# State-space recurrence of a hybrid encoder layer: one vector operation for both directions instead of two, and a lower pace of it beside keys, values and gate projections

## The chip, the cores and the metric

The kernel runs as one program on one core of a Trainium2 chip. Four engines matter here: TensorE (PE, matrix products, with its weight loads PEld), VectorE (DVE), ScalarE (ACT) and GpSimd (POOL); SyncE (SP) only issues transfers. The metric is the device time of one execution in microseconds; the median over several executions is compared.

## The reference, cut to what matters

One layer with 256 tokens and width 2048. Everything hangs on one input projection; the part that the change touches is the two-directional state-space recurrence (S5).

```python
h = rms_norm(x, mix_norm_g[l])
proj = h @ w_in[l]
q, k, v, u, gate_a, gate_b = jnp.split(proj, IN_SPLITS, axis=-1)
...
y_a = windowed_gqa(q, k, v, attn_sink[l]) @ w_attn_o[l]
ug = u.astype(jnp.float32).reshape(b_, s_, SSM_GROUPS, SSM_GROUP)
y_fwd = s5_direction(ug, ..., False)
y_bwd = s5_direction(ug, ..., True)
y_ssm = (y_fwd + y_bwd).reshape(b_, s_, SSM_WIDTH) + ssm_d[l] * ug.reshape(b_, s_, SSM_WIDTH)
y_act = jax.nn.gelu(y_ssm, approximate=False)
y_b = (y_act @ glu_w_a[l]) * jax.nn.sigmoid(y_act @ glu_w_b[l])
merged = jax.nn.sigmoid(gate_a) * y_a + jax.nn.sigmoid(gate_b) * y_b
x = x + merged @ w_out[l]
...
x = x + peer(h2, peer_w_query[l], ...)
```

Inside `s5_direction` every group has 64 complex states; a state at one time is a diagonal complex factor times the state before it, plus a driving term from `u`. The forward direction runs up the time axis, the other one down.

## The kernel before, in words

**Products.** All big weights are streamed from memory in pieces of 128x1024 (`raw`, four buffers). Each piece is split into a high part `whi` (ACT, `high_part`, line 151) and a low part `wlo` (DVE, `low_part`, line 136; two buffers each). `dense` (lines 284 to 288) then issues twelve products of 512 columns per piece: eight with `whi`, and four with `wlo`. I call the work on one such piece a half; eight halves make 512 columns of a weight matrix. The input projection has 16 such blocks, 128 halves: two of `u`, one of keys, one of values, four of queries, eight of gates. After it come the attention's output matrix (`w_ao`), the gated unit, `w_out`, the query projection of the expert layer, and two long passes over all experts.

**The recurrence.** Time is folded by two, so that 128 positions with 128 states per partition are left. The state tile is `X`, with index [direction][real, imaginary][32 groups][129 positions]; neighbours in a group index lie 129 words apart. `ssm` fills it (`ssm_bu`, 16 pairs of groups: transposes and products on PE, one half of the copies on ACT and one on DVE, line 612), and then makes 127 steps. In a step, for each direction: `s1` = state times real factor (`lr2`), `s2` = swapped state times imaginary factor (`li2`), then the new column gets `s1` and `s2` added. The trace calls both products `s`. One such operation has 64 elements per partition, two runs of 32 that hop 129 words from element to element. Eight such operations make a step, and the forward and backward ones alternate. Behind the steps the output products (lines 696 and 699, from `X`, `ccl` and `Tm`) make the state-space output, ACT applies the GELU, and POOL's queue moves it. The tile `ysp` then takes the place of `X` in memory: the split of the attention's result (`att_split`, tiles `attl` to `ysp`) has to wait until the last output product has read `X`, and `w_ao` needs that split.

**What sets the order.** The recurrence is a generator in the list `fill`. `dense` calls `pump(budget)` after each half: the budget is added to a credit, and generators are advanced until it is used up; a recurrence step costs 1.0. The budget is 2.5 in the blocks of `u`, `SPK` in those of keys and values, `SPU` = 1.2 in those of queries and `SPG` in those of gates. Ahead of the last gate block `drain` takes out whatever is left. That gives the order in which instructions are written; a scheduler then places them on each engine by priority and its own estimate of durations, the two splits of a weight piece 400 places earlier than written (`HP`). So the final order on an engine is not the written one. On each engine instructions start in that final order.

Of the kernel before, what the change touches and what calls it, by code (L numbers as in the profile page):

```python
# [17 lines left out]
OP = mybir.AluOpType  # L18
AX = mybir.AxisListType

P = 128
# [10 lines left out]
NG2 = 32  # L32
# [78 lines left out]
def _layer(ctx: ExitStack, tc: tile.TileContext, a, out):  # L111
# [17 lines left out]
    def mm_ps():  # L129
        return psm.tile([P, 512], F32, name="mm", tag="mm")  # L130

    def ax_ps():
        return psx.tile([P, 512], F32, name="ax", tag="ax")

    def tt(o, i0, i1, op, eng=None):
        return (eng or V).tensor_tensor(o, i0, i1, op=op)  # L136
# [10 lines left out]
    def act(o, i, f, **kw):  # L147
        S.activation(o, i, f, **kw)
# [36 lines left out]
    for i2 in range(2):  # L185
        for q in range(2):
# [4 lines left out]
                                      ap=[[0, P], [1, HEADS]]))  # L191
# [82 lines left out]
    def dense(w, cc, lh, ll, ps, budget=0.0, early=(), keep=False):  # L274

        nu = 2 * w.shape[1]
        parts = (p for m in range(nu // 2)
                 for p in split_units(unit(w, cc, m), early[m] if m < len(early) else ()))
        for un, (hi, lo) in enumerate(parts):
            kb = [(j, b) for j in range(2) for b in range(NB)]  # L280
            for j, b in kb:
                k = 2 * un + j
                h_, bs = hi[:, j * 512:(j + 1) * 512], slice(b * P, (b + 1) * P)
                PE.matmul(ps[b], lhsT=lh[:, k, bs], rhs=h_, start=(k == 0), stop=False)  # L284
                PE.matmul(ps[b], lhsT=ll[:, k, bs], rhs=h_, start=False, stop=False)  # L285
            for j, b in kb:
                k = 2 * un + j
                PE.matmul(ps[b], lhsT=lh[:, k, b * P:(b + 1) * P], rhs=lo[:, j * 512:(j + 1) * 512],  # L288
                          start=False, stop=(k == 2 * nu - 1))
            step()  # L290
            pump(budget)
        if keep:
            return
        flush()
# [7 lines left out]
    def tmp(shape, dt=F32, name="t8_"):  # L302
        return t8.tile(shape, dt, name=name, tag="t8")
# [60 lines left out]
    lr2 = ss.tile([P, 2, 2, NG2], F32, name="lr2")  # L364
    li2 = ss.tile([P, 2, 2, NG2], F32, name="li2")
# [122 lines left out]
    XW = P + 1  # L488
# [97 lines left out]
    def ssm_bu(X):  # L586
        ready = []
        for ip in range(17):
            if ip < 16:
                e, pl = ip // 2, ip % 2  # L590
                bp = ax_ps()
                for d in range(2):
                    for ri in range(2):
                        PE.transpose(bp[:, (2 * d + ri) * P:(2 * d + ri + 1) * P],
                                     bws[e][:, ri, d, 2 * pl:2 * pl + 2, :].rearrange("p i c -> p (i c)"), ident)
                bt = bts[ip % 2]
                for i2 in range(2):
                    hs = slice(i2 * 64, (i2 + 1) * 64)
                    copy(bt[i2][hs].rearrange("p k n -> p (k n)"), bp[hs])
                if pl == 1 and e < 8 - NBW:  # L600
                    load_bw()
                ready.append(bt)
            if ip > 0:
                for i2 in range(2):
                    i = 2 * (ip - 1) + i2
                    sp = ax_ps()
                    for k in range(4):
                        PE.matmul(sp[:, k * P:(k + 1) * P], lhsT=ready[ip - 1][i2][:, k, :], rhs=uT[:, ip - 1, :],
                                  start=True, stop=True)
                    spv = sp.rearrange("p (d r t) -> p d r t", d=2, r=2)  # L610
                    copy(X[:, 0, :, i, 1:1 + P], spv[:, 0])
                    V.tensor_copy(X[:, 1, :, i, 0:P], spv[:, 1])
            yield 0.5
# [26 lines left out]
    def ssm():  # L640
        Xf = pp.tile([P, XN], F32, name="X", tag="X")
        X = Xf.rearrange("p (d r i t) -> p d r i t", d=2, r=2, i=NG2)
        for d in range(2):
            nc.gpsimd.memset(X[:, d, :, :, d * P:d * P + 1], 0.0)
        yield from ssm_bu(X)
        dm = tmp([P, 16, P], name="dm")
        tt(dm, ident.unsqueeze(1).to_broadcast([P, 16, P]), dd.unsqueeze(2).to_broadcast([P, 16, P]), OP.mult)
        Tf = Tm.rearrange("p a b c -> p a (b c)")
        tt(Tf, Tf, dm, OP.add)
        yield 4.6  # L650
        base = X.offset
        pst = list(X.ap[0])
        SR = NG2 * XW

        def view(d, j, swap):
            return bass.AP(tensor=X.tensor, offset=base + 2 * d * SR + j + (SR if swap else 0),
                           ap=[pst, [-SR if swap else SR, 2], [XW, NG2]])

        s12 = ss.tile([P, 2, 2, 2, NG2], F32, name="s12")
        s1, s2 = s12[:, 0], s12[:, 1]  # L660
        ccl = []

        def load_cc():
            t_ = ss.tile([P, 2, 2, 4, 64], F32, name="ccl", tag="bw", bufs=NBW)
            nc.gpsimd.dma_start(t_.rearrange("p r d i c -> p (r d i c)"), cc_d[len(ccl)])
            ccl.append(t_)

        for _ in range(NBW):
            load_cc()
        for j in range(1, P):  # L670
            dirs = range(2)
            cu = [X[:, d, :, :, (j + 1, P - 1 - j)[d]] for d in dirs]
            pr_, sw = ([view(d, (j, P - j)[d], w_) for d in dirs] for w_ in (False, True))
            for d in dirs:
                tt(s1[:, d], pr_[d], lr2[:, d], OP.mult)
            for d in dirs:
                tt(s2[:, d], sw[d], li2[:, d], OP.mult)
            for d in dirs:
                tt(cu[d], cu[d], s1[:, d], OP.add)
            for d in dirs:  # L680
                tt(cu[d], cu[d], s2[:, d], OP.add)
            yield 1.0
        for _ in range(8):
            yield None
        Y = tmp([P, 16, P], name="Y")
        for e in range(8):
            cc_ = ccl[e]
            yp = ax_ps()
            for pl in range(2):
                ip = 2 * e + pl  # L690
                o = yp[:, pl * P:(pl + 1) * P]
                for i2 in range(2):
                    hs = slice(i2 * 64, (i2 + 1) * 64)
                    for n in range(4):
                        d, ri = n // 2, n % 2
                        PE.matmul(o[hs], lhsT=cc_[:, ri, d, 2 * pl + i2, :],
                                  rhs=X[:, d, ri, 2 * ip + i2, d:d + P], start=(n == 0), stop=False,
                                  tile_position=(0, i2 * 64), skip_group_check=True)
                PE.matmul(o, lhsT=Tm[:, ip].rearrange("p b c -> p (b c)"), rhs=uT[:, ip, :],
                          start=False, stop=True, skip_group_check=True)  # L700
            if e < 8 - NBW:
                load_cc()
            act(Y[:, 2 * e:2 * e + 2, :].rearrange("p a t -> p (a t)"), yp[:, :T], AF.Gelu)
            yield 2
        sp_ = pp.tile([P, 56, T], F32, name="ysp", tag="X")
        split.append(sp_)
        ya = sp_[:, 48:56, :]
        for i4 in range(4):
            for s_ in range(2):
                p0 = (i4 % 2) * 64 + s_ * 32  # L710
                nc.gpsimd.dma_start(ya[i4 * 32:(i4 + 1) * 32, :, s_ * P:(s_ + 1) * P],
                                  Y.rearrange("p (e q) t -> p e q t", q=2)[p0:p0 + 32, :, i4 // 2, :])
# [105 lines left out]
        nc.gpsimd.dma_start(att_d[:, g * 4 * T:(g + 1) * 4 * T], w2[:, 1])  # L818

    SPU = 1.2  # L820
    SPK = 1.8
    SPG = 2.2
    def values(ps):
        for b in range(NB):
            copy(vv[:, b, :], ps[b], scale=rstd[:, b:b + 1])
        yield

    def queries(g, ps):
        qT = tmp([P, 4, T], name="qT")
        yield from head_norm(ps, gq, qT)  # L830
        yield from attend(g, qT)

    for n in range(2 + KV):
        ps = [mm_ps(), mm_ps()]
        dense(a["w_in"], 2 + n, hh, hl, ps, SPK if n < 2 else SPU)
        front.append(head_norm(ps, gk, kT) if n == 0 else values(ps) if n == 1 else queries(n - 2, ps))
# [17 lines left out]
    for gi, dst in enumerate((sga_d, sgb_d)):  # L854
        for cc in range(4):
# [6 lines left out]
            ps = [mm_ps(), mm_ps()]  # L862
            dense(a["w_in"], 8 + gi * 4 + cc, hh, hl, ps, SPG)
            sg = tmp([P, NB, 512], name="sg")
# [27 lines left out]
    for cc in range(4):  # L892
# [11 lines left out]
        for b in range(NB):  # L904
            o = mg[b][:, cc * 512:(cc + 1) * 512]
# [9 lines left out]
    for cc in range(4):  # L915
# [3 lines left out]
        for b in range(NB):  # L919
            o = x1[b][:, cc * 512:(cc + 1) * 512]  # L920
# [32 lines left out]
    pr_ = ExitStack()  # L953
# [397 lines left out]
    for h in range(2):  # L1351
# [11 lines left out]
        for c in range(NK):  # L1363
# [41 lines left out]
            for i in range(8):  # L1405
                rh, rl = region(i)
                o = ot[:, i, NGT:]
# [29 lines left out]
```

## Time and profile before

| | us |
|---|---|
| median of 3 executions (2312.93 to 2314.45) | 2313.37 |
| the profiled execution, own time | 2316.0 |
| its span in the trace | 2314.2 |
| PE busy (share of the span) | 2242.6 (97%) |
| DVE busy | 1833.0 (79%) |
| ACT busy | 1218.2 (53%) |
| POOL busy | 312.5 (14%) |

Read the shares as averages over stages. PE is near its whole span in all of them, but a product that waits for its `wlo` shows only part of its wait as idle time, since products overlap; the distance from one half's last product to the next half's last product tells more than the busy share. DVE is far from busy in some stages and has no idle time at all in another.

### The profile page before, as it was taken

To read this page: it belongs to the slowest core of one execution; us is meant where nothing else is said; L and a number is where in the kernel's file an instruction comes from. 1 tells how busy PE (TensorE), PEld (TensorE's weight loads), DVE (VectorE), ACT (ScalarE), POOL (GpSimd) and SP (SyncE) were. 2 spreads that over 40 slices of the span, in tenths; PEclk is the share of its full clock that TensorE was granted. 3 is DMA by queue.
4 is the path that set the end of the run, shared out by engine and by line. 5 is a ranking of instruction groups with operands and counts; after the bars stand their busy time and mean duration, and the time that the engine had idled before them with its cause. 6 is when DMAs were issued, how large, how long until landed. Compare 5 with 4: busy or idle time off the path is not lost. (4 is left out here: it accounts for less than half of the span.)

```text
span 2314.2 us, 37265 instructions
## 1 busy us (share of the span) xinstructions
PE 2242.6 (97%) x13298; PEld 1996.1 (86%) x13298; DVE 1833.0 (79%) x4154; ACT 1218.2 (53%) x2090; POOL 312.5 (14%) x309
## 2 busy tenths in 40 slices
PE   7999899999999999999989999999999999999999
PEld 6788676678888888888879999999999999999998
DVE  7858999964466575999979999999778888875665
ACT  5885654334344554455445555555555555545554
POOL 3320000001000100000021222112323323200000
PEclk9999999999999999999999999999999999999999
DMA  6854345566666765555577677777888888876664
GB/s 236 263 186 137 128 137 170 171 224 193 223 204 203 239 214 188 178 191 185 186 244 247 241 243 252 248 241 258 291 319 305 300 313 306 290 229 218 206 209 156
DMA packets 145466, 519.05 MB, mean 224 GB/s; under 512 B 18032, under 2 KB 18656, under 8 KB 144896
## 3 DMA queue, kind: packets, MB, share of 16 engines
q1 hardware_dynamic: 113184, 410.04, 52.8%
q0 software_dynamic: 30944, 105.56, 13.0%
q8 instruction: 104, 1.70, 0.3%
q10 hardware_dynamic: 1152, 1.07, 0.1%
q14 instruction: 82, 0.67, 0.1%
HBM read 496.11 MB, written 18.87 MB: 223 GB/s over the span
## 5 line engine op out<-in xcount | busy, mean ns | idle before, releaser
L151 ACT ACTIVATE whi<-raw 128x1024 fp32r<-128x1024 f32 x768 | 814.6, 1061 | 933.4 <-PE mm L285 225.8
L136 DVE TENSOR_TENSOR wlo<-raw,whi 128x1024 fp32r<-128x1024 f32 x768 | 938.4, 1222 | 395.8 <-ACT whi L151 379.0
L1293 PE MATMUL mm<-h,whi 128*128 128x448 f32 x2048 | 478.9, 370 | 0.0
L1293 PEld LDWEIGHTS mm<-h,whi 128*128 128x128 f32 x2048 | 367.5, 190 | 22.7
L1300 PEld LDWEIGHTS mm<-h,wlo 128*128 128x128 f32 x2048 | 265.5, 191 | 33.2 <-DVE wlo L136 26.2
L1300 PE MATMUL mm<-h,wlo 128*128 128x224 f32 x2048 | 272.5, 275 | 14.4 <-DVE wlo L136 14.2
L1384 PE MATMUL mm<-wt,whi 128*128 128x448 f32 x1024 | 252.2, 367 | 4.0 <-DVE wt L136 4.0
L284 PE MATMUL mm<-whi,hb 128*128 128x512 f32 x512 | 204.4, 401 | 9.5 <-ACT hb L151 8.2
L285 PE MATMUL mm<-whi,hb 128*128 128x512 f32 x512 | 202.8, 398 | 0.3 <-DVE hb L145 0.2
L1384 PE MATMUL ax<-wt,whi 128*128 128x448 f32 x768 | 198.2, 365 | 0.0
L1384 PEld LDWEIGHTS mm<-wt,whi 128*128 128x128 f32 x1024 | 174.5, 190 | 15.1 <-issue 3.3
L1186 POOL DMA_INDIRECT rows<-in_down_rows_dram,rix x64 | 107.4, 1678 | 396.6 <-DVE dots L1194 389.4
L288 PE MATMUL mm<-wlo,hb 128*128 128x512 f32 x512 | 148.2, 406 | 10.1 <-DVE wlo L136 9.9
L1387 PE MATMUL ax<-wt,wlo 128*128 128x224 f32 x1024 | 156.8, 275 | 0.0
L1387 PE MATMUL mm<-wt,wlo 128*128 128x224 f32 x1024 | 156.4, 275 | 0.0
L1384 PEld LDWEIGHTS ax<-wt,whi 128*128 128x128 f32 x768 | 144.1, 188 | 10.2
L1387 PEld LDWEIGHTS mm<-wt,wlo 128*128 128x128 f32 x1024 | 144.9, 191 | 4.0
L1387 PEld LDWEIGHTS ax<-wt,wlo 128*128 128x128 f32 x1024 | 135.8, 193 | 0.0
L288 PEld LDWEIGHTS mm<-wlo,hb 128*128 128x128 f32 x512 | 92.9, 189 | 44.2 <-DVE wlo L136 26.3
L284 PEld LDWEIGHTS mm<-whi,hb 128*128 128x128 f32 x512 | 97.1, 190 | 32.0 <-ACT hb L151 8.6
L285 PEld LDWEIGHTS mm<-whi,hb 128*128 128x128 f32 x512 | 96.7, 190 | 20.3 <-DVE hb L145 1.1
L136 DVE TENSOR_TENSOR X<-X,s 128x64 f32<-128x64 f32 x508 | 107.1, 278 | 0.0
(276 smaller groups left out, 3224.0 us busy)
## 6 DMA issues: line engine op xcount, KB each, us to landing
raw<-in_down_dram SPq DMA_DIRECT2D x256, 512.0 KB
raw<-in_up_dram SPq DMA_DIRECT2D x256, 512.0 KB
raw<-in_w_in_dram SPq DMA_DIRECT2D x128, 512.0 KB
raw<-in_w_ao_dram SPq DMA_DIRECT2D x32, 512.0 KB
raw<-in_w_out_dram SPq DMA_DIRECT2D x32, 512.0 KB
raw<-in_w_q_dram SPq DMA_DIRECT2D x32, 512.0 KB
raw<-in_wgb_dram SPq DMA_DIRECT2D x16, 512.0 KB
raw<-in_wga_dram SPq DMA_DIRECT2D x16, 512.0 KB
```

The costliest lines, as they stand in the source:

```text
L136: return (eng or V).tensor_tensor(o, i0, i1, op=op)
L151: S.activation(o, i, AF.Copy, **kw)
L284: PE.matmul(ps[b], lhsT=lh[:, k, bs], rhs=h_, start=(k == 0), stop=False)
L285: PE.matmul(ps[b], lhsT=ll[:, k, bs], rhs=h_, start=False, stop=False)
L288: PE.matmul(ps[b], lhsT=lh[:, k, b * P:(b + 1) * P], rhs=lo[:, j * 512:(j + 1) * 512], start=False, stop=(k == 2 * nu - 1))
L1186: nc.gpsimd.indirect_dma_start(out=r[:PU], out_offset=None, in_=table, in_offset=bass.IndirectOffsetOnAxis(ap=rix[:PU, h, g:g + 1], axis=0))
L1293: PE.matmul(ps[:, :2 * ND], lhsT=hi[:, j * P:(j + 1) * P], rhs=h2[:, k].rearrange("p a t -> p (a t)"), start=(k == 0), stop=(k == KD - 1), ...
L1300: PE.matmul(ps[:, :ND], lhsT=lo[:, j * P:(j + 1) * P], rhs=h2[:, q * 8 + j, 0, :], start=False, stop=False, skip_group_check=True)
L1384: PE.matmul(acc[i][:, :2 * ND], lhsT=w_, rhs=wv, start=first, stop=False, skip_group_check=True)
L1387: PE.matmul(region(i)[0], lhsT=lo[:, i * P:(i + 1) * P], rhs=wh, start=False, stop=end, skip_group_check=True)
```

## The change

Each recurrence step is now four operations of 128 elements instead of eight of 64: `view` builds one access pattern over both directions (the forward column `j` and the backward column `P - j`, 128x2x64 in the order listings). The three arithmetic steps are the same. `SPK` goes from 1.8 to 1.5 and `SPG` from 2.2 to 1.7.

```diff
-        def view(d, j, swap):
-            return bass.AP(tensor=X.tensor, offset=base + 2 * d * SR + j + (SR if swap else 0),
-                           ap=[pst, [-SR if swap else SR, 2], [XW, NG2]])
+        def view(j, swap):
+
+            o = (j, P - j)
+            return bass.AP(tensor=X.tensor, offset=base + o[0] + (SR if swap else 0),
+                           ap=[pst, [2 * SR + o[1] - o[0], 2], [-SR if swap else SR, 2], [XW, NG2]])
...
         for j in range(1, P):
-            dirs = range(2)
-            cu = [X[:, d, :, :, (j + 1, P - 1 - j)[d]] for d in dirs]
-            pr_, sw = ([view(d, (j, P - j)[d], w_) for d in dirs] for w_ in (False, True))
-            for d in dirs:
-                tt(s1[:, d], pr_[d], lr2[:, d], OP.mult)
-            for d in dirs:
-                tt(s2[:, d], sw[d], li2[:, d], OP.mult)
-            for d in dirs:
-                tt(cu[d], cu[d], s1[:, d], OP.add)
-            for d in dirs:
-                tt(cu[d], cu[d], s2[:, d], OP.add)
+            cu, pr_, sw = view(j + 1, False), view(j, False), view(j, True)
+            tt(s1, pr_, lr2, OP.mult)
+            tt(s2, sw, li2, OP.mult)
+            tt(cu, cu, s1, OP.add)
+            tt(cu, cu, s2, OP.add)
             yield 1.0
...
     SPU = 1.2
-    SPK = 1.8
-    SPG = 2.2
+    SPK = 1.5
+    SPG = 1.7
```

The order on DVE in the middle of the gate blocks, from the 101st `wlo` on (`s_2058` is the scratch tile of both products, `li_143` and `lr_142` are the factors; "waits DVE" is a wait for an earlier result of DVE itself). Before:

```order
L136 TENSOR_TENSOR wlo<-raw,whi 128x1024 [waits DMAHW4_49,PE_49,Activation_49]
L136 TENSOR_TENSOR s_2058<-X,li_143 128x64
L136 TENSOR_TENSOR X<-X,s_2058 128x64 [waits DVE_49] x4
L136 TENSOR_TENSOR s_2058<-X,lr_142 128x64 [waits DVE_49] x2
L136 TENSOR_TENSOR s_2058<-X,li_143 128x64 x2
L136 TENSOR_TENSOR X<-X,s_2058 128x64 [waits DVE_49] x4
L136 TENSOR_TENSOR wlo<-raw,whi 128x1024 [waits DMAHW5_49,PE_49,Activation_49]
```

The same place of the changed kernel (scratch tile `s_2207`):

```order
L136 TENSOR_TENSOR wlo<-raw,whi 128x1024 [waits DMAHW4_49,PE_49,Activation_49]
L136 TENSOR_TENSOR s_2207<-X,li_143 128x128
L136 TENSOR_TENSOR X<-X,s_2207 128x2x64 [waits DVE_49] x2
L136 TENSOR_TENSOR s_2207<-X,lr_142 128x128 [waits DVE_49]
L136 TENSOR_TENSOR s_2207<-X,li_143 128x128
L136 TENSOR_TENSOR X<-X,s_2207 128x2x64 [waits DVE_49]
L136 TENSOR_TENSOR wlo<-raw,whi 128x1024 [waits DMAHW5_49,PE_49,Activation_49]
L136 TENSOR_TENSOR X<-X,s_2207 128x2x64 [waits DVE_49]
```

About one and a half steps stand between two `wlo` in both. What moved is the neighbourhood: an addition to `X` now stands right behind the addition whose result it reads, and the next step's product right behind that; before, an operation of the other direction stood between.

The order on PE where the recurrence hands over to the output products (`ax<-X,ccl`; `mm<-wlo,hb` are the four last products of a half of the input projection). Before:

```order
L288 MATMUL mm<-wlo,hb 128x512 [waits DVE_49]
L288 MATMUL mm<-wlo,hb 128x512 x3
L696 MATMUL ax<-X,ccl 64x128 [waits DMASW1_49,DVE_49,Pool_49]
L696 MATMUL ax<-X,ccl 64x128
L696 MATMUL ax<-X,ccl 64x128 [waits DVE_49,Pool_49]
L696 MATMUL ax<-X,ccl 64x128 x5
L699 MATMUL ax<-uT,Tm 128x128
```

In the changed kernel (eight products with `whi` are cut to their first and last here by the "..." line):

```order
L288 MATMUL mm<-wlo,hb 128x512 x2
L692 MATMUL ax<-X,ccl 64x128 [waits DMASW1_49,DVE_49,Pool_49]
L288 MATMUL mm<-wlo,hb 128x512
L284 MATMUL mm<-whi,hb 128x512 [waits Activation_49]
...
L285 MATMUL mm<-whi,hb 128x512
L692 MATMUL ax<-X,ccl 64x128 [waits DVE_49]
L692 MATMUL ax<-X,ccl 64x128 [waits Pool_49]
L692 MATMUL ax<-X,ccl 64x128 x5
L695 MATMUL ax<-uT,Tm 128x128
```

Counted from the start, 118 halves stand ahead of the first output product before, and 123 halves and the eight `whi` products of the next one ahead of the second output product now; the eight groups of output products have two halves mixed in before and stand in one run now. The recurrence's first step stands behind the 39th `wlo` on DVE before and behind the 43rd now; its last step behind the 119th before and behind the 125th now. Behind `w_ao` the orders of both kernels are the same again.

## Rows read from the trace of the kernel before

**Rows 1.** The page: busy us of each engine.

```profile
PE 2242.6 (97%) x13298; PEld 1996.1 (86%) x13298; DVE 1833.0 (79%) x4154; ACT 1218.2 (53%) x2090; POOL 312.5 (14%) x309
```

**Rows 2.** Stretches: length, busy PE PEld DVE ACT POOL (instructions), clock, DMA.

```profile
190.40:380.00 189.60, 172.48 (x744) 131.33 (x743) 188.58 (x787) 108.72 (x250) 4.29 (x8) 0.98 0.40 136
380.00:495.40 115.40, 105.44 (x419) 75.47 (x417) 115.40 (x456) 41.86 (x43) 3.21 (x6) 1.00 0.52 175
495.40:553.60 58.20, 58.20 (x410) 48.49 (x410) 23.28 (x36) 21.78 (x34) 10.03 (x18) 1.00 0.65 217
553.60:640.00 86.40, 86.40 (x383) 71.57 (x382) 43.49 (x40) 34.47 (x35) 5.36 (x10) 1.00 0.69 225
```

**Rows 3.** DVE in order of time, gate blocks: start, us, instruction, count.

```profile
489.63 1.20 DVE L136 TENSOR_TENSOR wlo<-raw,whi 128x1024 fp32r<-128x1024 f32 x1
490.76 0.79 DVE L136 TENSOR_TENSOR X<-X,s 128x64 f32<-128x64 f32 x4
491.48 0.43 DVE L136 TENSOR_TENSOR s<-X,lr 128x64 f32<-128x64 f32 x2
...
492.90 0.25 DVE L136 TENSOR_TENSOR s<-X,lr 128x64 f32<-128x64 f32 x1
493.08 1.20 DVE L136 TENSOR_TENSOR wlo<-raw,whi 128x1024 fp32r<-128x1024 f32 x1
```

**Rows 4.** PE in order of time: last four products of two neighbouring halves, twice.

```profile
487.62 1.19 PE L288 MATMUL mm<-wlo,hb 128*128 128x512 f32 x4 [0.43 <-DVE wlo L136]
...
490.89 1.19 PE L288 MATMUL mm<-wlo,hb 128*128 128x512 f32 x4 [0.25 <-DVE wlo L136]
...
541.78 1.07 PE L288 MATMUL mm<-wlo,hb 128*128 128x512 f32 x4
...
544.50 1.07 PE L288 MATMUL mm<-wlo,hb 128*128 128x512 f32 x4
```

**Rows 5.** DVE groups by form, 0 to 820 us: busy, mean ns, idle before.

```profile
L136 DVE TENSOR_TENSOR X<-X,s 128x64 f32<-128x64 f32 x508 | 107.1, 278 | 0.0
L136 DVE TENSOR_TENSOR s<-X,lr 128x64 f32<-128x64 f32 x254 | 58.4, 270 | 0.0
...
L136 DVE TENSOR_TENSOR prm<-prm 128x64 f32<-128x64 f32 x24 | 5.0, 221 | 0.1
```

**Rows 6.** DVE in order of time, parameters: chain of three, then two independent ones.

```profile
25.21 0.74 DVE L145 SCALAR_TENSOR_TENSOR prm<-prm 128x64 f32<-128x64 f32 x3
...
51.16 0.22 DVE L136 TENSOR_TENSOR prm<-prm 128x64 f32<-128x64 f32 x1
51.29 0.22 DVE L136 TENSOR_TENSOR prm<-lam,prm 128x64 f32<-128x64 f32 x1
...
55.51 0.29 DVE L136 TENSOR_TENSOR stg<-stg 128x128 f32<-128x128 f32 x1
55.71 0.29 DVE L145 SCALAR_TENSOR_TENSOR stg<-stg 128x128 f32<-128x128 f32 x1
```

**Rows 7.** DVE in order of time, expert pass: a hopping operation and its successor.

```profile
1302.24 0.68 DVE L136 TENSOR_TENSOR A<-A,ax 128x260 f32<-128x260 f32 x1
1302.82 1.23 DVE L136 TENSOR_TENSOR wlo<-raw,whi 128x1024 fp32r<-128x1024 f32 x1
```

**Rows 8.** DVE groups by form, 1300 to 2000 us: busy, mean ns, idle.

```profile
L136 DVE TENSOR_TENSOR A<-A,ax 128x124 f32<-128x124 f32 x1 | 0.4, 394 | 0.0
...
L136 DVE TENSOR_TENSOR A<-A,ge 128x128 f32<-128x128 f32 x2 | 0.6, 287 | 0.0
```

**Rows 9.** In order of time: `Tm`, first step, first output product, first of `w_ao`.

```profile
152.41 2.29 DVE L136 TENSOR_TENSOR Tm<-Tm,dm 128x2048 f32<-128x2048 f32 x1 [5.32 <-DMA Tm<-stg]
...
190.39 0.44 DVE L136 TENSOR_TENSOR s<-X,lr 128x64 f32<-128x64 f32 x2
...
495.46 1.58 PE L696 MATMUL ax<-X,ccl 128*64 128x128 f32 x16
...
553.57 0.39 PE L284 MATMUL mm<-whi,ysp 128*128 128x512 f32 x1
```

## The prediction, made before the changed kernel ran

> **What bounds the kernel now.** I read the page's busy times first: PE is busy for 97% of the span [rows 1], so a change on DVE can only help where PE waits for DVE. I then cut the span into stretches [rows 2]. From the first recurrence step to the first output product, 190.4 to 495.4 us, DVE has next to no idle time (188.58 of 189.6 us, 115.40 of 115.4), while PE makes 744 and 419 products. Right behind it, in 553.6 to 640, the same kind of product runs at 383 in 86.4 us, that is 226 ns each; in 380 to 495.4 it is 275 ns. The granted clock is 0.98 and 1.00 there, so the clock is not the reason. In PE's order of time the distance from one half to the next is 490.89 - 487.62 = 3.27 us with a wait for `wlo` in front, and 544.50 - 541.78 = 2.72 us where DVE has time [rows 4]. So the input projection's middle is bound by DVE, about 0.6 us in each gate half, and from 495.46 on PE sets the end: the first product of `w_ao` comes at 553.57 [rows 9] without a gap, and nothing behind it differs between the kernels. What I have to find is when that product starts now.
>
> **What one operation costs.** In the gate blocks a step runs from 491.48 to 492.90 us, 1.42 us, and the four additions before it take 491.48 - 490.76 = 0.72 [rows 3]: eight operations, so 0.176 us from start to start. Each lasts 270 to 278 ns by itself [rows 5]; neighbours overlap by about 0.1. The overlap ends when an operation reads what the one in front of it wrote. In the chain of three, (0.74 - 0.22) / 2 = 0.26 us lie between two starts; the same size without such a wait starts 51.29 - 51.16 = 0.13 later [rows 6]. A direct dependence costs 0.13 us.
>
> The price of 128 hopping elements isn't in the trace. Contiguous operations go from 0.13 us at 64 elements to 55.71 - 55.51 = 0.20 at 128 and 490.76 - 489.63 = 1.13 at 1024 [rows 3, 6], that is 0.069 us plus 1.04 ns an element. The hopping one has 0.176 at 64. If the extra 0.04 us belongs to the operation, 128 elements cost 0.176 + 0.064 = 0.240 us; if it belongs to the elements, (0.176 - 0.069) / 64 = 1.67 ns each, they cost 0.282. A third row reads and writes with a hop of 224 words: 260 elements take 1302.82 - 1302.24 = 0.58 us [rows 7], 1.97 ns each, which gives 0.321. That one also reads another memory (`ax` lies in PSUM), and its hop is another. That the extra grows with the elements is shown by the forms: 124 hopping elements last 394 ns, 128 contiguous ones 287 [rows 8], twice the 57 ns by which 278 exceeds 221 at 64 [rows 5]. I take 0.282, worked out from the recurrence's own operations, and keep 0.240 and 0.321 as ends.
>
> **The recurrence, before and after.** Up to the first output product DVE makes 126 of the 127 steps before: 1008 x 0.176 = 177.4 us. Now the second output product waits for the last step, since its wait for DVE stands behind that step in the order: 508 x 0.282 = 143.3 us. Each step has two direct dependences, addition behind addition and next product behind that, 253 in all. In the order on DVE something else (mostly a `wlo` or a piece of a head norm) stands between 64 of the pairs; 189 x 0.13 = 24.6 us remain. Together 167.9, a gain of 9.5 us. So halving the operations gives little: about 34 us come off, and 25 go back into waits that the other direction used to fill.
>
> **What else moves on DVE between the first step and that product.** 82 `wlo` instead of 79, 3 x 1.13 = +3.4; `dm` and `Tm` fall into the stretch, as long as the row of `Tm` [rows 9] less the overlap, 2 x 2.2 = +4.4; four more gate pieces and one head norm fewer, about -1, an estimate. Sum +6.8. The stretch was 495.46 - 190.39 = 305.1 us [rows 9]; now 305.1 + 6.8 - 9.5 = 302.4.
>
> **When it starts.** The lower `SPK` puts four more halves ahead of the first step (43 `wlo` instead of 39). PE is the bound there, so 4 x 2.72 = 10.9 us later: 201.3. The head norm of the first query group, a chain of small operations that read each other, now stands ahead of the last four copies into `X`; I add 2 us for it, between 0 and 4. Start 203.3, end 505.7.
>
> **What PE has left then.** Before, from 495.46 to 553.57: 58.1 us for ten halves and the output products. Now 123 halves and two thirds of one are done instead of 118: 5.67 x 2.72 = 15.4 us less, so 42.7. The first product of `w_ao` starts at 548.4 instead of 553.57, **5.2 us earlier**. Halves in the stretch are paid either at PE's price or hidden behind DVE; both kernels have DVE full over it, since 1.5 steps x about 1.32 + 1.13 = 3.1 us a half is still over 2.72. That is why the lower pace alone is worth nearly nothing here: the order has about 1.5 steps between two `wlo` in both kernels, because the scheduler, not the budget, spaces them while DVE has a backlog.
>
> At the hand-over the split of the attention's result must wait for the last output product. Behind that only 4.3 halves, 11.8 us, are left as cover, eight halves before. The split's first quarter needs one ACT copy and one DVE subtraction of the size of a `wlo`, some 2.5 us. I cost it at nothing; without cover it would be up to 5 us. What is late next is then the state-space output's way through POOL's queue; 32 halves of `w_ao` hide it.
>
> The sum is made on the profiled execution, 2316.0 us with a span of 2314.2, 2.6 above the median. 5.2 us less are 2310.8 there, and **2308.2** on the median.
>
> **The rivals.**
> *The element price is higher.* At 0.321 us an operation the recurrence costs 508 x 0.039 = 19.8 us more, 14.6 us slower in all: 2328. It decides at 0.292 (no change) and 0.301 (slower by over 0.2%). For it speaks the only other hopping row [rows 7]; against it, that this row reads PSUM, and that both kinds of recurrence operation, one with a hop on one side and one on two, cost the same at 64.
> *The pieces cancel.* With an operation at 0.288 to 0.300, or a start two microseconds later still, the sum is within 0.2%: about 2313.
> The Trainium skill has a rule on this, "Vector Engine (DVE) Microarchitecture Reference", section 5.2 "Measured stream behaviour on trn2": about 75 ns an instruction, 1.04 ns a column, and 1.71 to 1.76 when a source or the destination hops on every element. By that 128 elements would cost an estimated 0.296 us and the change would come out 2 us slower, that is no change; at 64 it gives 186 ns where the rows show 176.
> *The extra belongs to the operation.* At 0.240 us, 508 x 0.042 = 21.3 us come off besides: 2287. The forms speak against it [rows 8].
> *The wait isn't paid.* If the additions overlapped in spite of the dependence, 24.6 us more: 2284. The chain of three speaks against it [rows 6].
> *The hand-over isn't covered.* 5 us given back: 2313.
>
> **How the numbers follow.** The forecast, with an operation between 0.270 and 0.288 us, has 0.45: 2302 to 2311, and 2308 as its number. Cancelling or an uncovered hand-over 0.24; the higher price 0.21; the two cheap cases together 0.10, mostly part of the way. Faster by over 0.2%, 4.6 us, about what a measurement of this kernel can tell from no change: 0.41 of the forecast's 0.45 and the cheap cases, 0.50. Within: 0.04 and 0.23, 0.27. Slower: 0.23. The range leaves out the far half of the cheap cases and of the dear one: 2296 to 2322.
>
> **What would show it.** DVE's groups by form: 508 operations of 128 elements with a mean near 0.38 us. In order of time, a step without anything between at 4 x 0.282 + 0.26 = 1.39 us, with visible gaps of about 0.03 in front of the second addition and the next product, and starts 0.41 apart there. The gate halves on PE at 3.1 to 3.2 us instead of 3.3. The first output product that waits near 506 us, `w_ao` near 548. I am wrong if the two starts around a pair of neighbours lie over 0.30 apart, if the step is over 1.45 us, if DVE shows idle time between 203 and 505, or if PE waits for ACT in front of `w_ao`.

## The result and the profile after

The changed kernel takes 2331.2 us (median of 5 runs, 2325.48 to 2332.22), beside 2314.45 for the kernel before (5 runs, 2312.93 to 2318.48). The ratio is 1.0062 with a 95% interval of 1.005 to 1.0075: **slower by 0.6%**. The forecast was 2308.2, its range ended at 2322. The profiled execution has a span of 2329.5 us, 15.3 more than before.

The page's busy times in the changed kernel, to be read against [rows 1]:

```profile
PE 2249.5 (97%) x13298; PEld 2000.2 (86%) x13298; DVE 1834.9 (79%) x3646; ACT 1217.1 (52%) x2090; POOL 310.8 (13%) x309
```

DVE issues 508 instructions less and is busy for as long as before. The windows of the changed kernel, by the stretches of [rows 2] and with one of six microseconds at the end of the recurrence (length, busy PE, PEld, DVE, ACT, POOL with instructions, clock, DMA share, GB/s):

```profile
190.40:380.00 189.60, 171.34 (x756) 131.15 (x756) 182.15 (x467) 107.95 (x248) 4.85 (x9) 0.97 0.40 131
380.00:495.40 115.40, 101.83 (x408) 73.65 (x407) 111.17 (x237) 40.76 (x43) 4.30 (x8) 1.00 0.53 175
520.00:526.00 6.00, 6.00 (x26) 4.17 (x26) 2.49 (x5) 1.17 (x2) 0.00 (x0) 0.61 0.59 196
553.60:640.00 86.40, 86.40 (x392) 71.64 (x392) 49.32 (x51) 39.63 (x46) 11.15 (x20) 1.00 0.72 228
```

From 380 to 495.4 us PE makes 408 products where it made 419. DVE shows idle time now, 4.2 us in that stretch and 7.4 in the one before, though nothing else bounds it: 237 instructions with gaps took the place of 456 without. Behind the stretch PE is as full as before.

DVE's groups by form, which answer to [rows 5] (busy, mean ns of one, idle before):

```profile
L136 DVE TENSOR_TENSOR X<-X,s 128x128 f32<-128x128 f32 x254 | 100.6, 396 | 6.6
L136 DVE TENSOR_TENSOR s<-X,lr 128x128 f32<-128x128 f32 x127 | 49.3, 388 | 3.5
L136 DVE TENSOR_TENSOR s<-X,li 128x128 f32<-128x128 f32 x127 | 48.3, 380 | 0.0
```

There are 508 operations with a mean near 0.39 us; their busy time is 198.2 us, and with half the instructions it fell only from some 224 (107.1 and twice 58.4, [rows 5]). What decides is the distance from one start to the next. DVE in order of time in the changed kernel, at the first step and in the gate blocks, and its last operation on `X`:

```profile
199.76 0.39 DVE L136 TENSOR_TENSOR s<-X,lr 128x128 f32<-128x128 f32 x1
200.07 0.38 DVE L136 TENSOR_TENSOR s<-X,li 128x128 f32<-128x128 f32 x1
200.48 0.83 DVE L136 TENSOR_TENSOR X<-X,s 128x128 f32<-128x128 f32 x2
201.34 0.39 DVE L136 TENSOR_TENSOR s<-X,lr 128x128 f32<-128x128 f32 x1
...
471.95 0.39 DVE L136 TENSOR_TENSOR s<-X,lr 128x128 f32<-128x128 f32 x1
472.26 0.38 DVE L136 TENSOR_TENSOR s<-X,li 128x128 f32<-128x128 f32 x1
472.67 0.40 DVE L136 TENSOR_TENSOR X<-X,s 128x128 f32<-128x128 f32 x1
472.98 1.21 DVE L136 TENSOR_TENSOR wlo<-raw,whi 128x1024 fp32r<-128x1024 f32 x1
...
522.60 0.38 DVE L136 TENSOR_TENSOR X<-X,s 128x128 f32<-128x128 f32 x1
```

A step without anything between takes 201.34 - 199.76 = 1.58 us; the forecast was 1.39, and before it was 1.42 [rows 3]. Three distances of the four are long. Product to product is 0.31 us. Second product to first addition is 0.41, although the addition reads what the first product wrote, not the second: **this wait isn't in the forecast.** The two additions (0.83 us for both, 0.40 each) start some 0.43 apart, and the next product comes as far behind the second of them; the forecast had 0.41 for these two. Where a `wlo` follows instead, it starts 0.31 behind its neighbour (472.67 to 472.98).

PE in order of time, to be read against [rows 4, 9]: the last four products of two neighbouring halves, then the hand-over, then the first product of `w_ao`:

```profile
443.41 1.19 PE L288 MATMUL mm<-wlo,hb 128*128 128x512 f32 x4 [0.42 <-DVE wlo L136]
446.86 1.21 PE L288 MATMUL mm<-wlo,hb 128*128 128x512 f32 x4 [0.43 <-DVE wlo L136]
...
519.97 0.66 PE L692 MATMUL ax<-X,ccl 128*64 128x128 f32 x2 [3.63 <-issue]
520.56 0.80 PE L288 MATMUL mm<-wlo,hb 128*128 128x512 f32 x1
521.16 0.63 PE L284 MATMUL mm<-whi,hb 128*128 128x512 f32 x1
...
524.70 1.36 PE L692 MATMUL ax<-X,ccl 128*64 128x128 f32 x14
...
567.12 0.39 PE L284 MATMUL mm<-whi,ysp 128*128 128x512 f32 x1
```

A gate half takes 446.86 - 443.41 = 3.45 us; the forecast was 3.1 to 3.2, and it was 3.27 before. The first output products stand between the products of a half and wait 3.63 us; the row names no releaser, but the additions of the last step but one end on DVE at 519.88 us, just ahead of them. Behind this wait the granted clock is 0.61 on average from 520 to 526 us, for the most part the lower level of 1.2 GHz, and a product of 512 columns takes 0.63 instead of 0.39 us until 524.7. The first product of `w_ao` comes at 567.12, 13.55 us later than before and 18.7 later than forecast.

### The profile page after: what moved, and what is told of

It reads as the page before. It is cut to its first block, busy times and chain, and to the rows that moved or that the text cites. A ratio compares the mean times of both kernels' runs of the same rounds, so it can differ in the third digit from the quotient of the medians.

```text
span 2329.5 us, 36764 instructions
## 1 busy us (share of the span) xinstructions
PE 2249.5 (97%) x13298; PEld 2000.2 (86%) x13298; DVE 1834.9 (79%) x3646; ACT 1217.1 (52%) x2090; POOL 310.8 (13%) x309
## 5 line engine op out<-in xcount | busy, mean ns | idle before, releaser
L136 DVE TENSOR_TENSOR X<-X,s 128x128 f32<-128x128 f32 x254 | 100.6, 396 | 6.6
```

## The experiments

Theory A, formed on this trace: the loss lies in the recurrence itself, an operation costs 0.30 us by itself and three of its four neighbours wait. Against it stand the pace (a later start, the hand-over at a low clock) and the pattern over both directions as such.

**The two halves of the change, each alone.** `fuse_only` is the changed kernel with `SPK = 1.8` and `SPG = 2.2`; `pace_only` is the kernel before with

```diff
-    SPK = 1.8
-    SPG = 2.2
+    SPK = 1.5
+    SPG = 1.7
```

Expected of the first: 

> One operation for both directions, with the pace of before (1.8 and 2.2). Theory A: the time goes to the recurrence itself, since a 128-element operation costs 0.31 us and three of its four neighbours in a step wait for each other. Then DVE's stretch is about as much longer than before as in the changed kernel (323.2 against 305.1 us, less the 6.8 us of other work that the lower pace moved in: some 11 us), and since DVE starts at 190 and PE has the full ten halves left behind it, the time is 8 to 14 us over before: 2322 to 2328. Theory B: the later start and the hand-over at the clock's dip are what costs; then this kernel shows the forecast's gain of the recurrence, about 2305.

Expected of the second: 

> The two operations for two directions of before, with the lower pace (1.5 and 1.7). Theory A: the later start is paid back by fewer halves behind the stretch, so within 4 us of before: 2311 to 2318. Theory B: the pace is the loss, and this kernel comes out like the changed one: 2326 to 2332.

`fuse_only` took 2323.12 us (ratio 1.0034, 1.0021 to 1.0048), `pace_only` 2317.66 (1.0012, 1.0003 to 1.0021). In order of time in `fuse_only`, first step on DVE, first output product and first product of `w_ao` on PE:

```profile
188.13 0.39 DVE L136 TENSOR_TENSOR s<-X,lr 128x128 f32<-128x128 f32 x1
...
504.70 1.58 PE L692 MATMUL ax<-X,ccl 128*64 128x128 f32 x16
...
562.81 0.39 PE L284 MATMUL mm<-whi,ysp 128*128 128x512 f32 x1
```

and the same three in `pace_only`:

```profile
200.59 0.43 DVE L136 TENSOR_TENSOR s<-X,lr 128x64 f32<-128x64 f32 x2
...
510.49 2.10 PE L696 MATMUL ax<-X,ccl 128*64 128x128 f32 x16 [3.48 <-issue]
...
556.46 0.39 PE L284 MATMUL mm<-whi,ysp 128*128 128x512 f32 x1
```

With the pace of before, the fused operation alone moves the first product of `w_ao` by 562.81 - 553.57 = 9.2 us; DVE starts 2.3 us earlier, the stretch is 316.6 us long instead of 305.1, and PE's part behind it is 58.1 as before. The pace alone moves it by 2.9: DVE starts 10.2 us later, the stretch is 4.8 longer, and PE's part is 12.1 shorter. Together 12.1 of the 13.55. Theory A takes most of the loss, the pace a small part. In the medians the two alone make 11.8 us (8.65 and 3.19) of the changed kernel's 16.75; the rest shows only with both together, and no run splits it up.

**Waits, or the pattern?** `groups` keeps the changed kernel's views over both directions, but cuts each operation into two halves of the 32 groups (the expectations call them heads). `view` gets the half `h` as a third argument, and `hs` are the slices of the halves:

```diff
...
-            tt(s1, pr_, lr2, OP.mult)
-            tt(s2, sw, li2, OP.mult)
-            tt(cu, cu, s1, OP.add)
-            tt(cu, cu, s2, OP.add)
+            for h in range(2):
+                tt(s1[:, :, :, hs[h]], view(j, False, h), lr2[:, :, :, hs[h]], OP.mult)
+            for h in range(2):
+                tt(s2[:, :, :, hs[h]], view(j, True, h), li2[:, :, :, hs[h]], OP.mult)
+            for h in range(2):
+                tt(cu[h], cu[h], s1[:, :, :, hs[h]], OP.add)
+            for h in range(2):
+                tt(cu[h], cu[h], s2[:, :, :, hs[h]], OP.add)
```

> The changed kernel, but each of its four operations is cut by groups of heads instead of by direction: eight operations of 64 elements over both directions, so that an operation never reads what the one right in front of it wrote. Theory A (waits between neighbours): starts 0.18 us apart as before, a clean step at 1.40 to 1.45 us, and the time that of the lower pace alone, 2311 to 2318. Theory C (the pattern over both directions, with three steps instead of two, is itself dear): starts at 0.20 us or more, a step over 1.55 and a time of 2328 or more.

It took 2317.8 us (1.0013, 1.0004 to 1.0022), no other than the pace alone. DVE in order of time in `groups`, first step and one later piece:

```profile
198.07 0.45 DVE L136 TENSOR_TENSOR s<-X,lr 128x64 f32<-128x64 f32 x2
198.44 0.44 DVE L136 TENSOR_TENSOR s<-X,li 128x64 f32<-128x64 f32 x2
198.80 0.80 DVE L136 TENSOR_TENSOR X<-X,s 128x64 f32<-128x64 f32 x4
199.51 0.43 DVE L136 TENSOR_TENSOR s<-X,lr 128x64 f32<-128x64 f32 x2
...
202.40 0.44 DVE L136 TENSOR_TENSOR s<-X,li 128x64 f32<-128x64 f32 x2
202.88 0.64 DVE L136 TENSOR_TENSOR X<-X,s 128x64 f32<-128x64 f32 x3
```

The step is 1.44 us, with starts 0.18 apart: the pattern over both directions costs nothing at 64 elements, and theory C falls. At some steps the first addition waits here too (202.40 to 202.88 is 0.48 for two operations instead of 0.36).

**The third wait.** `via_tile` lets the first addition write to a tile of its own, `s3`:

```diff
...
-            tt(cu, cu, s1, OP.add)
-            tt(cu, cu, s2, OP.add)
+            tt(s3, cu, s1, OP.add)
+            tt(cu, s3, s2, OP.add)
```

> The changed kernel, but its first addition writes to a tile of its own and the second adds from there into X, so the first addition no longer writes into the tensor that the product in front of it reads. Theory A with a wait of a writer for the reader in front of it: product to first addition goes from 0.41 to 0.31 us, a clean step from 1.58 to 1.48, and with some 80 to 127 uncovered steps 8 to 12 us come back: 2319 to 2323. Rival: the third wait has nothing to do with X being read; then 0.41 stays and the time is that of the changed kernel, 2329 to 2333.

It took 2317.15 us (1.0011, 1.0002 to 1.002), 14.05 less than the changed kernel. DVE in order of time in `via_tile`, one step:

```profile
248.44 0.39 DVE L136 TENSOR_TENSOR X<-s,s 128x128 f32<-128x128 f32 x1
248.86 0.39 DVE L136 TENSOR_TENSOR s<-X,lr 128x128 f32<-128x128 f32 x1
249.17 0.38 DVE L136 TENSOR_TENSOR s<-X,li 128x128 f32<-128x128 f32 x1
249.47 0.38 DVE L136 TENSOR_TENSOR s<-X,s 128x128 f32<-128x128 f32 x1
249.88 0.39 DVE L136 TENSOR_TENSOR X<-s,s 128x128 f32<-128x128 f32 x1
```

Second product to first addition is 0.30 us now, the step 249.88 - 248.44 = 1.44. The mechanism came as expected; the gain is larger than the 8 to 12 us, partly because the scheduler put other pieces in between (75 `wlo` stand between its first and last operation of the recurrence, 82 in the changed kernel); this run alone doesn't part the wait from the order.

Two further kernels, profiled once each, ask why the addition waits. `other_tile` runs the first addition in place on a small tile (`tt(s3, s3, s1, OP.add)`); `no_feedback` sends both additions to tiles of their own (`tt(s3, cu, s1, OP.add)`, `tt(s4, cu, s2, OP.add)`). The first leaves the product `s1` out of the state, the second leaves out the recurrence.

> The changed kernel, but the first addition runs in place on a small tile of its own (with a hop of two elements) instead of on X; its sum is left out of the result. It tells two readings of the third wait apart. If a writer of X waits for the product in front of it that reads X: product to first addition starts 0.31 us apart. If an addition in place waits by itself: 0.41 stays.

> The changed kernel, but both additions write to tiles of their own, so that X isn't updated: the recurrence itself is left out, and no operation of a step reads what the one in front of it wrote or writes what it read. It measures the price of a 128-element operation by itself. Theory A (0.31 us by itself, the rest of the 1.58 us step is waits): starts 0.30 to 0.31 us apart everywhere, a clean step of 1.22 us, some 30 us less on DVE than in the changed kernel and a time near 2300. Rival (an addition on this pattern costs over 0.40 by itself): the starts in front of and between the additions stay at 0.41 to 0.44, a step of 1.5 or more.

DVE in order of time in `other_tile`:

```profile
308.86 0.38 DVE L136 TENSOR_TENSOR s<-X,li 128x128 f32<-128x128 f32 x1
309.15 0.29 DVE L136 TENSOR_TENSOR s<-s,s 128x128 f32<-128x128 f32 x1
309.35 0.39 DVE L136 TENSOR_TENSOR X<-X,s 128x128 f32<-128x128 f32 x1
```

and in `no_feedback`:

```profile
304.58 0.43 DVE L136 TENSOR_TENSOR s<-X,lr 128x128 f32<-128x128 f32 x1
304.88 0.43 DVE L136 TENSOR_TENSOR s<-X,li 128x128 f32<-128x128 f32 x1
305.18 0.74 DVE L136 TENSOR_TENSOR s<-X,s 128x128 f32<-128x128 f32 x2
305.79 0.43 DVE L136 TENSOR_TENSOR s<-X,lr 128x128 f32<-128x128 f32 x1
```

In place on another tile the addition starts 0.29 us behind the product: being in place isn't the cause. Where no operation needs the one right in front of it, a step takes 305.79 - 304.58 = 1.21 us, **0.30 us an operation**, also where each of them still reads single elements of `X` at hops. So here theory A holds in both points. The time of `no_feedback`, 2310.87 us, missed the expectation of near 2300; `other_tile`, of which no time was expected, took 2305.62, beside 2315.74 for before. The scheduler, given other waits, placed only 67 (`other_tile`) and 61 (`no_feedback`) `wlo` among the steps instead of 82. `no_feedback` had its last product of the recurrence at 452.77, and then DVE stood idle 1.5 us a half for ACT, with halves at the 2.72 us that PE takes by itself, while PE had made only 742 products from 190.4 to 380 us, where the changed kernel has 756. That this order is the whole of the miss was not tested.

**The hop.** `sum_first` is the kernel before with its pace, but adds the products to each other first:

```diff
             for d in dirs:
-                tt(cu[d], cu[d], s1[:, d], OP.add)
+                tt(s1[:, d], s1[:, d], s2[:, d], OP.add)
             for d in dirs:
-                tt(cu[d], cu[d], s2[:, d], OP.add)
+                tt(cu[d], cu[d], s1[:, d], OP.add)
```

> The kernel before with its pace and its eight operations, but the two products are added to each other first (contiguous, in place) and their sum is added to X then: two of eight operations without a hop. If the hop is what an operation costs above 0.135 us: 2 x 0.041 us x 126 steps = 10 us less on DVE in the stretch where it bounds, 2303 to 2307. Rival: the price of the small operation does not depend on the hop, or the new dependence shows: 2312 to 2318.

2305.91 us, ratio 0.9958 (0.9944 to 0.9971): **faster than before by 0.4%**, as expected. The group by form in `sum_first` shows the additions that became contiguous, two of eight operations a step:

```profile
L136 DVE TENSOR_TENSOR s<-s 128x64 f32<-128x64 f32 x254 | 45.7, 214 | 0.0
```

`time_outer` is the kernel before with `X` laid out by time first, so that no operation of a step has a hop:

```diff
-        X = Xf.rearrange("p (d r i t) -> p d r i t", d=2, r=2, i=NG2)
+        X = Xf.rearrange("p (t d r i) -> p d r i t", d=2, r=2, i=NG2)
...
-            return bass.AP(tensor=X.tensor, offset=base + 2 * d * SR + j + (SR if swap else 0),
-                           ap=[pst, [-SR if swap else SR, 2], [XW, NG2]])
+            return bass.AP(tensor=X.tensor, offset=base + 4 * NG2 * j + 2 * NG2 * d + (NG2 if swap else 0),
+                           ap=[pst, [-NG2 if swap else NG2, 2], [1, NG2]])
```

> The kernel before with its pace and its eight operations, but X laid out with time outermost, so that all operations of a step read and write neighbouring elements; the hop moves to the copies into X and to the output products' right-hand operand. If the hop is the price: starts 0.135 us apart, a step of 1.08 instead of 1.40, 40 us less on DVE, gate halves near PE's 2.72 us, and 2275 to 2290. Rival: the copies (32 on DVE, as many on ACT) or the output products (512-byte hop) get slower by about as much, or the small operations keep 0.176: 2305 or more.

2298.27 us, 0.9929 (0.9915 to 0.9942): faster, but by less than the some 40 us that DVE saved (its last operation of the recurrence ends at 456.5 us instead of 498.1). PE's groups by form in `time_outer`, 430 to 570 us, say where the rest went:

```profile
L696 PE MATMUL ax<-X,ccl 128*64 128x128 f32 x256 | 49.5, 435 | 0.0
```

In the kernel before these 256 products take 25.3 us, 278 ns each. The hop went to PE, which sets the end there, and 24.2 us went with it; the time lies between the two forecasts.

`pair` puts two groups side by side at each time, `quad` four; the copies into `X` and the output products' operand are indexed to match:

```diff
-        X = Xf.rearrange("p (d r i t) -> p d r i t", d=2, r=2, i=NG2)
+        X = Xf.rearrange("p (d r i t q) -> p d r i q t", d=2, r=2, i=NG2 // 2, q=2)
...
-            return bass.AP(tensor=X.tensor, offset=base + 2 * d * SR + j + (SR if swap else 0),
-                           ap=[pst, [-SR if swap else SR, 2], [XW, NG2]])
+            return bass.AP(tensor=X.tensor, offset=base + 2 * d * SR + 2 * j + (SR if swap else 0),
+                           ap=[pst, [-SR if swap else SR, 2], [2 * XW, NG2 // 2], [1, 2]])
```

> The kernel before with its pace, its order and its eight operations, but X laid out so that two heads lie side by side at every time: the recurrence reads and writes pairs of neighbours with a hop between pairs, and the copies and the output products see a hop of 8 bytes. If a hop costs only where each element stands by itself (the in-place addition with a hop of 8 bytes started 0.20 us before its follower, like a contiguous one): starts 0.135 us apart, a step of 1.08, output products at 278 ns as before, PE bound by itself from the first step on, first product of w_ao near 513 and 2270 to 2280. Rival: a run of two is still a hop for one of the engines: 0.176 us on DVE (2310 or more) or output products at 435 ns (2295 to 2300).

> As with pairs, but four heads side by side: the copies and the output products see a hop of 16 bytes. If what counts is two elements within 16 bytes, the recurrence keeps 0.135 us an operation, but the output products go to 435 ns as with time outermost: near 2297. If a hop of 16 bytes is still free for PE: as with pairs.

`pair` took 2275.9 us, ratio 0.9828 (0.9814 to 0.9841): **faster than both kernels**, with the eight operations of the kernel before. In order of time in `pair`, two starts of a step on DVE, then PE:

```profile
189.23 0.35 DVE L136 TENSOR_TENSOR s<-X,lr 128x64 f32<-128x64 f32 x2
190.31 0.35 DVE L136 TENSOR_TENSOR s<-X,lr 128x64 f32<-128x64 f32 x2
...
453.52 1.64 PE L697 MATMUL ax<-X,ccl 128*64 128x128 f32 x16
...
512.69 0.39 PE L284 MATMUL mm<-whi,ysp 128*128 128x512 f32 x1
```

its PE group, and behind it that of `quad`:

```profile
L697 PE MATMUL ax<-X,ccl 128*64 128x128 f32 x256 | 26.4, 283 | 0.0
```

```profile
L697 PE MATMUL ax<-X,ccl 128*64 128x128 f32 x256 | 47.1, 408 | 0.0
```

The step is 1.08 us, the output products keep their price (283 ns), the first product of `w_ao` comes 40.9 us earlier than before, and the time is 40.3 shorter. With four side by side DVE is as quick, but PE reads with a hop of 16 bytes at 408 ns, and its one run took 2295.2. The Trainium skill, "Vector Engine (DVE) Microarchitecture Reference", section 5.2 "Measured stream behaviour on trn2 (trn3 not measured)", says that a port runs at full rate only while its elements come in aligned runs of at least two words, and that any hop between such runs is free. The starts 0.135 us apart in `pair` agree. The "only" does not hold here: in `other_tile` the first addition reads and writes 128 single elements 8 bytes apart, and the operation behind it starts 0.20 us later (309.15 to 309.35), as behind a contiguous one. The Trainium skill, "SBUF — State Buffer", section "Door 1: The DMA port swizzle (why `[64,N]` ≈ `[32,N]`)", names lines of 16 bytes, each of which needs at least two accesses for full rate. PE's 283 ns at a hop of 8 bytes and 408 at 16 agree, and so does that 0.20 us; the same passage goes on to "4 fp32" as the stride that is free, and if that means a step of four elements, the 408 ns speak against it.

`pair_pace` is `pair` with the lower pace, `outer_fused` the changed kernel on the layout of `time_outer`.

> The layout in pairs with the lower pace (1.5 and 1.7). If PE alone sets the time there, the pace has nothing to move: within 3 us of the pairs with the pace of before, 2273 to 2279. Rival: the later start makes the last step late for the output products and PE waits there: 2280 or more.

> The changed kernel (one operation for both directions, lower pace) on the layout with time outermost, so without a hop. It asks whether the operation for both directions pays once the hop is gone. Theory A (three waits on neighbours a step): 0.20 us from the first product to the second, 0.33 at the other three places, a step of 1.20 us against 1.08 of the eight operations on the same layout; DVE stays the bound and the time is over that of the eight operations: 2302 to 2314. Rival (without a hop the operation for both directions saves its fixed part): a step under 1.05 and a time of 2293 to 2300.

`pair_pace` took 2275.38 us (0.9831, 0.9818 to 0.9845): where PE bounds, the pace moves nothing. `outer_fused` took 2298.24 in its one run, as `time_outer` does with eight operations. That is the rival's time, not theory A's, but PE is busy for all of 380 to 495.4 us in both (115.40 and 115.39 us), so the time can't tell their steps apart. DVE in order of time in `outer_fused`:

```profile
202.14 0.29 DVE L136 TENSOR_TENSOR s<-X,lr 128x128 f32<-128x128 f32 x1
202.35 0.28 DVE L136 TENSOR_TENSOR s<-X,li 128x128 f32<-128x128 f32 x1
202.56 0.61 DVE L136 TENSOR_TENSOR X<-X,s 128x128 f32<-128x128 f32 x2
203.20 0.29 DVE L136 TENSOR_TENSOR s<-X,lr 128x128 f32<-128x128 f32 x1
```

Theory A was wrong here in one point: the third wait isn't there. Product to first addition is 0.21 us, though the addition updates the same `X` that the product reads, and the step is 1.06 us instead of 1.20, beside 1.08 in `time_outer` (191.67 to 192.75). So a writer of `X` doesn't wait for a reader of it as such. The built programs, which list each instruction's waits, show what does: these waits are written into the program, DVE waits for its own count of finished operations.

```
                 first additions that wait for the second product, of 127
after            127
fuse_only        127
groups            43
via_tile           8
outer_fused        8
```

In `groups` the first of a step's two is counted. Also counted are those behind an operation that itself waits for as much: 2 in the changed kernel, all 8 in each of the last two. In the changed kernel, then, every first addition starts behind a wait for the second product's count; where they wait for the first product alone, 0.30 us (0.20 without a hop) is what stands in the trace. Why the program sets this wait with one layout of `X` and not with the other, that is how it judges whether the columns of two steps overlap, was not tried.

## Why the prediction was wrong

**What bounds the kernel: right.** DVE bounds the stretch and the start of `w_ao` carries the time: in the eight kernels timed over several rounds, that product and the median move together (`pair` -40.9 and -40.3 us, `sum_first` -8.0 and -9.8, `time_outer` -16.8 and -17.5, `fuse_only` +9.2 and +8.7). In the changed kernel they are further apart, +13.55 and +16.75; 1.8 us of that lie behind the product in the profiled execution (15.3 in all) and are not explained.

**What one operation costs: the step that failed first.** "I take 0.282", the forecast said, from 64 elements at 0.176; `no_feedback` shows 0.30. Per added element that is (0.30 - 0.176) / 64 = 1.94 ns, not 1.67: almost the 1.97 of the row with the other hop [rows 7], which the forecast kept as an end and set aside. 508 x 0.018 = 9.1 us. That is the upper end of the rival "the pieces cancel" (0.288 to 0.300 us, no change); the third wait took the sum beyond it. The rule of the Trainium skill that the forecast cites there ("Vector Engine (DVE) Microarchitecture Reference", section 5.2 "Measured stream behaviour on trn2 (trn3 not measured)") gave an estimated 0.296 and was the nearest. The cheap end, 0.240, should have been 0.243 (64 x 1.04 ns is 0.067 us, not 0.064); nothing hangs on it.

**The recurrence: right in two waits, a third not seen.** 189 uncovered pairs were counted, and the order of the changed kernel has 189 neighbours (88 and 101). They cost 0.43 - 0.30 = 0.13 us, as forecast. The step that failed here is "each step has two direct dependences". It left out the wait of the first addition for the second product: 101 such neighbours at 0.41 - 0.30 = 0.11 us are 11.1. The listing ahead of the prediction does show first additions that wait for DVE, in both kernels; what it doesn't say is whose count they wait for. Price and third wait together, 20.2 us, make up nearly all of the 20.8 by which the stretch from the first step to the last addition (199.76 to 522.98, 323.2 us) exceeds the forecast 302.4; another 0.45 us is a wait of the last `wlo` for PE, at 521.45. Either one alone would have brought the sum near +4 to +6 us instead of -5.2.

**What else moves on DVE: right,** with 82 `wlo` as forecast. **The start: 3.5 us too late.** The first step is at 199.76 instead of 203.3, so neither the 2 us for the head norm nor the full 10.9 for the four halves came. This error ran against the others and made the miss smaller.

**What PE has left: right but for 1.4 us.** From the end of the recurrence to `w_ao` it is 567.12 - 522.98 = 44.1 us, forecast 42.7. The eight products behind PE's wait, which the forecast had as done by then, take 3.54 us at the low clock (521.16 to 524.70, 0.44 each where it is 0.23 otherwise) and end 1.7 us behind the last addition. All of it: -3.5 + 20.8 + 1.4 = 18.7 us at `w_ao`.

**The pace alone, worth nearly nothing: right**, +0.12% by itself. **The split's cover: right**; PE doesn't wait in front of `w_ao`.

**The rivals.** The dear element came nearest, with its mechanism and its sign. It gave 2328 by 0.321 us alone; in truth 0.30 and the third wait share the loss. It had a chance of 0.21, although the forecast named 0.292 as the price of no change and had the one other hopping row beyond that. "The wait isn't paid" is refuted. Of the signs that were to show it wrong, three came: neighbours 0.31 us apart where 0.30 was the bound (read for neighbours without a wait, since the forecast itself had 0.41 for those with one), a step over 1.45, and DVE idle within the stretch.

## What to carry to other kernels

Two independent chains on one in-order engine cover each other's waits; merged into one operation, they give back in waits what the halved count saves: the fused step breaks even at best here (1.06 against 1.08 us without a hop, 1.44 against 1.42 with one), and one more wait made it a loss. Before counting dependences from the formulas, read the built program's waits, since the program may set one that the data don't need. And look at the layout before the count of operations: two neighbours at a time on DVE, without giving PE a hop of 16 bytes, brought 1.7%, where halving the operations brought nothing.

## What was not expected of the hardware

- PE's 128-column float32 products depend on the hop of the moving operand: 278 ns contiguous, 283 with a hop of 8 bytes, 408 with 16, 435 with 512.
- A copy out of PSUM into `X` on DVE, 256 elements, takes 424 ns with its target contiguous or at a hop of 8 bytes, 627 with 16 and 622 with 512. An addition on 128 single elements 8 bytes apart costs 0.20 us from start to start, a contiguous one as much (`other_tile`, [rows 6]).
- A wait of DVE for its own neighbour costs 0.11 to 0.14 us at 64 and at 128 elements, with a hop and without (128 with a hop: 0.41 to 0.44 against 0.30; without: 0.31 and 0.33 against 0.21; 64 with a hop: 0.30 against 0.18 in `groups`; without: 0.26 against 0.13 in [rows 6]).
